# Gate and up groups with three, four or five seven-product pairs, the fifth pair kept in tiles of later activations

## The chip, the cores and the metric

The kernel runs on one core of a Trainium2 chip. The metric is device time in microseconds (us). Three runs before the change took 2402.5, 2402.4 and 2402.98 us; their median is 2402.5 us.

## The reference, cut to what matters

The program is a two-layer decoder trunk on 256 tokens with 2048 features in float32: a retention layer and an MLA layer, each followed by a SwiGLU block. The change touches only the first product of SwiGLU:

```
def swiglu(x, w_gu, w_down):
    gate, up = jnp.split(x @ w_gu, [D_FF], axis=-1)      # x: 256 x 2048, w_gu: 2048 x 11264
    return (jax.nn.silu(gate) * up) @ w_down              # D_FF = 5632
```

## The kernel before, in words

Every float32 operand is split into a rounded part (`hi`) and a remainder (`lo`), both in a format that TensorE takes at full speed, and a product is the sum of three matmuls: hi by hi, hi by lo, lo by hi. ScalarE writes `hi` (a cast, L210), VectorE subtracts to get `lo` (L211).

The gate and up product of a layer runs in 11 groups, j = 0 to 10. A group takes 512 columns of gate and 512 of up against all 2048 rows of the weight, which are 16 row tiles of 128, and writes four banks of PSUM: two token halves (t = 0, 1) by two column halves. In the plain form each row tile costs 2 x 2 x 3 = 12 matmuls of 512 columns. Two neighbouring row tiles and the two column halves are a 2 x 2 block product, and for some such pairs of row tiles the Strassen-Winograd form is used: seven block products in place of eight, so 21 matmuls in place of 24, for four more additions of weights on VectorE and four of activations. Group 0 is plain. Groups 1 to 10 go through `first_sevens` with `GU_SEVENS` = 4: pairs 0 to 3 (row tiles 0 to 7) with seven products, row tiles 8 to 15 plain.

`first_sevens` makes, for each pair p, four weight operands: `b` (b00 beside the sum t2, L458 and L459, cast and subtracted in two halves of 512), `a` (the sums ta, L458 and L462, 1024), `c` (the pair's second row tile as loaded, 1024) and `d` (t2 plus a block, L473, 512; two pairs share one tile). TensorE walks them in four loops: per pair b, b, a, a; then c on bank b00; then c on bank b01; then d on bank b10. Between loop one and loop three VectorE turns the banks around: u = b01 + copy of b00 (L485), v = b10 + u (L488), b01 = b11 - u (L492), b11 = b11 - copy of v (L495). The products of c on b01 must wait for L492.

Casts and remainders lie in two rings of five tiles each (tags `whi`, `wlo`, WB = 5); a sixth operand can only be cast when TensorE has used up the first. Row tiles as loaded lie in four `raw` tiles (the first row tile of a pair, s0, and the plain row tiles) and four `y4` tiles (the second row tile of a pair, s1). All loads of 512 KB each are issued by SyncE (the SP queue), in order: one whose buffer is not free holds up those behind it.

The block's activations lie in 11 tiles of tag `aT`, one per group, each written after its group. Until then `spare_a` lends them out: `share(slots, room)` gives a group up to two raw tiles (names with `xraw`) and up to two hi/lo pairs (`xhi`, `xlo`) for its last row tiles, fewer when fewer slots are left.

The left operands of the pairs (sums of activations, L246 to L249 and a split) are made during group 0 by `watched`, when the transposed input of both token halves is there; they are kept for all groups of the layer. The order on each engine is set when the program is built, by the tile framework's scheduler, and the engines follow it in order.

The lines that matter below: L450, L453, L555 (loads of s0, s1, plain row tiles), L456 (t2), L458 to L463 (sums and splits of b and a), L468 (c), L473 (d), L481 and L489 (copies of banks by ScalarE), L485 to L495, L419 (all matmuls), L1005 (`share`).

Of the kernel before, what the change touches and what calls it, by code (L numbers as in the profile page):

```python
# [8 lines left out]
F32 = mybir.dt.float32  # L9
F32R = mybir.dt.float32r  # L10
# [5 lines left out]
P = 128  # L16
SEQ = 256
D = 2048
DT = D // P
# [12 lines left out]
NG = 104  # L32


GU_SEVENS = 4
DN_SEVENS = (2, 5, 7, 10, 12, 15, 17), (2, 4, 5, 7, 10, 12, 15, 17)
RTO_SEVENS = (3, 6, 9, 12), (3, 5, 6, 9, 12)
MLO_SEVENS = (3, 5), (1, 3)
# [20 lines left out]
def trunk(  # L59
# [362 lines left out]
                )  # L422
                begun.add(bank)

    def first_sevens(lhs, kts, w, g, name, n, left, spare):

# [18 lines left out]
        def begin(p):  # L447
            step()
            raw = wp.tile([P, 1024], F32, tag="raw", bufs=RAW, name=f"{name}_s0")
            nc.sync.dma_start(out=raw, in_=w[g, 2 * p])  # L450
            step()
            raw1[p] = r1 = sb.tile([P, 1024], F32, tag="y4", bufs=4, name=f"{name}_s1")
            nc.sync.dma_start(out=r1, in_=w[g, 2 * p + 1])  # L453
            b00, b01, b11 = raw[:, 0:512], raw[:, 512:1024], r1[:, 512:1024]
            ta = tp7.tile([P, 1024], F32, tag="tsum", bufs=2, name=f"{name}_ta")
            t2[p] = wp.tile([P, 512], F32, tag="mv", bufs=MV, name=f"{name}_t2")  # L456
            b, a = parts("b"), parts("a")
            nc.vector.tensor_add(out=ta[:, 0:512], in0=b00, in1=b01)  # L458
            nc.vector.tensor_add(out=t2[p], in0=ta[:, 0:512], in1=b11)  # L459
            split(*half(b, 0), b00)  # L460
            split(*half(b, 1), t2[p])
            nc.vector.tensor_add(out=ta[:, 512:1024], in0=b01, in1=b11)  # L462
            split(*a, ta)  # L463
            wt["b", p], wt["a", p] = b, a
# [116 lines left out]
    def watched(pairs):  # L581


        made, held, tiles = {}, {}, [None]

        def seen(t, k0, n, part):
            for p in range(pairs):
                if k0 <= 2 * p < k0 + n:
                    held[t, p] = part[:, 2 * p - k0], part[:, 2 * p - k0 + 1]
                    if (1 - t, p) in held:  # L590
                        f, hi, lo = tiles[0](len(made))
                        left_sums(*held[0, p], *held[1, p], f, hi, lo)
                        made[p] = hi, lo

        watch[0] = seen
        return made, tiles
# [167 lines left out]
    def retention():  # L764
# [43 lines left out]
        with tc.tile_pool(name="rt_s", bufs=1) as sp:  # L808
# [88 lines left out]
            with tc.tile_pool(name="rt_v", bufs=1) as rp:  # L897
# [63 lines left out]
                    for t in range(NT):  # L961
                        later(2 + t, lambda h=h, t=t, pr=(ph, pl), v=(vh, vl), sg=sg: mixed(h, t, pr, v, sg))

                gu_next[0] = watched(GU_SEVENS)
                closing(
                    take_y, RH * 4, ret_out, g_mix_post[0], G_FFN, "rto",
                    lambda name: rp.tile([P, 1024], F32, tag="sg", bufs=1, name=name), sevens=RTO_SEVENS,
# [3 lines left out]
    def swiglu(i):  # L971
        with tc.tile_pool(name=f"ff{i}", bufs=1) as fp:
# [19 lines left out]

            def sums(n):
                f = wp.tile([P, 4, P], F32, tag="mv", bufs=MV, name=f"sf{i}")
                if n < 2:
                    hi = fp.tile([P, 4, P], F32R, tag="sa", bufs=4, name=f"sh{i}")
                    lo = fp.tile([P, 4, P], F32R, tag="sa", bufs=4, name=f"sl{i}")
                else:
                    hi = wp.tile([P, 4, P], F32R, tag="ah", bufs=3, name=f"sh{i}")
                    lo = wp.tile([P, 4, P], F32R, tag="al", bufs=3, name=f"sl{i}")  # L1000
                return f, hi, lo
# [3 lines left out]

            for j in range(groups):
                name = f"gu{i}_{j}"
                spare = share(groups - j, spare_a)
                if j:
                    banks = first_sevens(  # L1010
                        h_lhs, DT, w_gu[i], j, name, GU_SEVENS, lambda p: ins[p], spare
                    )
                else:
                    banks = group(h_lhs, DT, tile_load(w_gu[i], j, name, 0, spare), name, lead=4)
# [17 lines left out]
    def mla():  # L1032
        with tc.tile_pool(name="ml", bufs=1) as mp:
# [152 lines left out]
            with tc.tile_pool(name="ml_a", bufs=1) as ap:  # L1186
# [110 lines left out]
                for hp in range(AH // 2):  # L1297
                    if hp:
                        qb = pair_products(hp)
                    attention(hp, qb)  # L1300
                gu_next[0] = watched(GU_SEVENS)
                closing(
                    lambda k0, n: oT[:, k0 : k0 + n], AH, mla_out, g_mix_post[1], G_FFN + DT, "mlo",
                    lambda name: ap.tile([P, 1024], F32, tag="aqkT", bufs=1, name=name), sevens=MLO_SEVENS,
# [98 lines left out]
```

## Time and profile before

| what | value |
|---|---|
| profiled execution, own time | 2400.07 us |
| its span, first to last instruction | 2398.3 us |
| median of the three runs | 2402.5 us |
| granted TensorE clock, mean | 0.999 |
| TensorE busy (matmuls) | 2382.3 us, 99% |
| VectorE busy | 2179.7 us, 91% |
| ScalarE busy | 1500.3 us, 63% |

Times in the trace count from the first instruction of the span. A matmul's recorded time is longer than the distance to the next one, since they are pipelined; distances between starts are what counts. In a timeline, a row with `xN` merges N instructions, and the bracket names the idle time of the engine before the row and what ended it.

### The profile page before, as it was taken

Reading aid. Unit: us, or ns where it says so; the run is one execution under the profiler, and the core shown is the slowest. Engines: PE = TensorE matmul, PEld = TensorE weight load, DVE = VectorE, ACT = ScalarE, POOL = GpSimd, SP = SyncE. Lnnn points to the kernel's source line nnn. Section 1 sums busy time; section 2 is a strip of 40 time slices with the busy share of each in tenths; the row PEclk is TensorE's granted clock in tenths of the full one; section 3 lists DMA queues with packets and bytes.
Section 4 is the critical chain, followed back from the end, with each engine's and each line's share of the span. In section 5 each row is a group of like instructions: output and inputs, shape, how many; then the busy total and the mean of one; then the engine's idle time right before and its main releaser. Section 6 shows DMA issues by size and latency. Waiting matters only on the chain.

```text
span 2398.3 us, 30805 instructions
## 1 busy us (share of the span) xinstructions
PE 2382.3 (99%) x10843; PEld 1971.0 (82%) x10843; DVE 2179.7 (91%) x3112; ACT 1500.3 (63%) x2126; POOL 28.5 (1%) x38
## 2 busy tenths in 40 slices
PE   9999999999999999999999999999999999999998
PEld 7888888888888888888888888887888888888887
DVE  8899888888899999999988987889999999998998
ACT  6555665665666656666666666656666665666664
POOL 0000000000000000000000000000100000000000
PEclk9999999999999999999999999999999999999999
DMA  8555465545656665656456655445666565645655
GB/s 285 187 195 191 167 212 184 170 170 192 206 194 219 207 207 199 209 179 219 161 197 210 200 196 158 129 138 171 234 205 216 177 218 184 212 167 183 221 199 168
DMA packets 129611, 463.76 MB, mean 193 GB/s; under 512 B 14640, under 2 KB 15024, under 8 KB 129456
## 3 DMA queue, kind: packets, MB, share of 16 engines
q1 hardware_dynamic: 129456, 461.80, 57.7%
q8 instruction: 85, 1.39, 0.2%
q14 instruction: 70, 0.57, 0.1%
HBM read 459.64 MB, written 2.10 MB: 193 GB/s over the span
## 4 chain that ended last, share of the span: by engine, by line
PE 94%; DVE 4%; DMA 1%; issue 1%; ACT 1%; SPq 0%; POOL 0%; DVEq 0%; POOLq 0%; ACTq 0%
PE gu_b L419 37%; PE dn_b L419 15%; PE rvg_b L419 14%; PE rqk_b L419 6%; PE rto_b L419 6%; PE q L419 3%; PE dn_m L419 3%; PE mlo_b L419 2%; PE mc_b L419 1%; PE rto_m L419 1%; PE ftp L988 1%; PE ry L916 1%; PE htp L602 0%; PE rsc L861 0%; PE asc L1240 0%
## 5 line engine op out<-in xcount | busy, mean ns | idle before, releaser
L419 PE MATMUL gu_b<-gu_w_hi,hT 128*128 128x512 f32 x1296 | 353.6, 391 | 0.1
L419 PEld LDWEIGHTS gu_b<-gu_w_hi,hT 128*128 128x128 f32 x1296 | 242.3, 188 | 50.6 <-DVE hT L211 0.9
L210 ACT CAST dn_w_hi<-dn_w_raw 128x1024 fp32r<-128x1024 f32 (+1 forms) x176 | 169.1, 978 | 78.4 <-DMA dn_w_raw<-w_down 33.7
L419 PE MATMUL gu_b<-gu_w_lo,hT 128*128 128x512 f32 x648 | 200.4, 391 | 0.0
L211 DVE TENSOR_TENSOR dn_w_lo<-dn_w_raw,dn_w_hi 128x1024 fp32r<-128x1024 f32 (+1 forms) x176 | 193.8, 1130 | 7.1 <-ACT dn_w_hi L210 6.3
L419 PE MATMUL rvg_b<-rvg_w_hi,hT 128*128 128x512 f32 x576 | 157.4, 391 | 0.0
L419 PE MATMUL dn_b<-dn_w_lo,dn_ah 128*128 128x512 f32 x494 | 156.7, 390 | 0.3 <-DVE dn_w_lo L211 0.3
L419 PE MATMUL dn_b<-dn_w_hi,dn_ah 128*128 128x512 f32 x494 | 156.7, 390 | 0.0
L419 PE MATMUL dn_b<-dn_w_hi,dn_al 128*128 128x512 f32 x494 | 156.7, 390 | 0.0
L211 DVE TENSOR_TENSOR gu_w_lo<-gu_w_raw,gu_w_hi 128x1024 fp32r<-128x1024 f32 x122 | 143.6, 1223 | 6.0 <-ACT gu_w_hi L210 6.0
L419 PEld LDWEIGHTS gu_b<-gu_w_lo,hT 128*128 128x128 f32 x648 | 121.2, 188 | 26.3 <-DVE gu_w_lo L211 1.5
L210 ACT CAST gu_w_hi<-gu_w_raw 128x1024 fp32r<-128x1024 f32 x122 | 122.5, 1049 | 29.2 <-PE gu_b L419 11.3
L419 PEld LDWEIGHTS rvg_b<-rvg_w_hi,hT 128*128 128x128 f32 x576 | 107.7, 188 | 22.0
L210 ACT CAST gu_ahi<-gu_ta 128x1024 fp32r<-128x1024 f32 x80 | 84.4, 1055 | 46.7 <-PE gu_b L419 36.0
L211 DVE TENSOR_TENSOR gu_clo<-gu_s,gu_chi 128x1024 fp32r<-128x1024 f32 x80 | 97.6, 1222 | 14.7 <-ACT gu_chi L210 13.4
L419 PEld LDWEIGHTS dn_b<-dn_w_lo,dn_ah 128*128 128x128 f32 x494 | 92.7, 188 | 19.8 <-DVE dn_w_lo L211 0.7
L419 PEld LDWEIGHTS dn_b<-dn_w_hi,dn_ah 128*128 128x128 f32 x494 | 92.8, 188 | 19.2
L419 PEld LDWEIGHTS dn_b<-dn_w_hi,dn_al 128*128 128x128 f32 x494 | 92.8, 188 | 19.2
L211 DVE TENSOR_TENSOR gu_alo<-gu_ta,gu_ahi 128x1024 fp32r<-128x1024 f32 x80 | 97.8, 1223 | 7.0 <-ACT gu_ahi L210 6.9
L210 ACT CAST gu_bhi<-gu_s 128x512 fp32r<-128x512 f32 x80 | 49.7, 622 | 81.6 <-PE gu_b L419 65.9
L419 PE MATMUL rqk_b<-rqk_w_hi,hT 128*128 128x512 f32 x352 | 99.4, 396 | 1.2 <-ACT rqk_w_hi L210 1.1
L210 ACT CAST gu_chi<-gu_s 128x1024 fp32r<-128x1024 f32 x80 | 83.8, 1051 | 13.6 <-PE gu_b L419 13.4
(535 smaller groups left out, 6284.9 us busy)
## 6 DMA issues: line engine op xcount, KB each, us to landing
dn_w_raw<-w_down SPq DMA_DIRECT2D x176, 512.0 KB, 4.5
gu_s<-w_gu SPq DMA_DIRECT2D x160, 512.0 KB, 4.6
gu_w_raw<-w_gu SPq DMA_DIRECT2D x152, 512.0 KB, 3.7
rvg_w_raw<-ret_vg SPq DMA_DIRECT2D x67, 512.0 KB, 4.4
rto_w_raw<-ret_out SPq DMA_DIRECT2D x64, 512.0 KB, 4.3
rvg_s<-ret_vg SPq DMA_DIRECT2D x48, 512.0 KB, 4.2
rqk_w_raw<-ret_qk SPq DMA_DIRECT2D x43, 512.0 KB, 4.3
gu_w_xraw<-w_gu SPq DMA_DIRECT2D x40, 512.0 KB, 5.2
```

Source lines behind the costliest of these rows:

```text
L210: nc.scalar.copy(out=hi, in_=src)
L211: nc.vector.tensor_sub(out=lo, in0=src, in1=hi.bitcast(F32))
L419: nc.tensor.matmul(out, e[2](), e[3](), start=bank not in begun, stop=ends[bank, added.get(bank, 0)] == n, skip_group_check=bank in added,)
L916: nc.tensor.matmul(y, left, right, start=n == 0, stop=n == len(terms) - 1)
L988: nc.tensor.transpose(tp[:, b * P : (b + 1) * P], a[:, b * P : (b + 1) * P], ident)
```

## The change

`GU_SEVENS` becomes a list by group: none in group 0, three pairs in group 1, then 5, 4, 5, 4, 5, 4, 4, 4, 4. Over a layer's groups 1 to 10 that is 42 pairs where there were 40. In a group with five pairs, the second row tile and t2 of pair 4 lie in `aT` tiles, and so do the left operands of pair 4, from group 0 until group 6. `kept` takes these out of what `share` may lend.

```diff
-GU_SEVENS = 4
+GU_SEVENS = 0, 3, 5, 4, 5, 4, 5, 4, 4, 4, 4
...
-    def first_sevens(lhs, kts, w, g, name, n, left, spare):
+    def first_sevens(lhs, kts, w, g, name, n, left, spare, fifth=None):
...
-            raw1[p] = r1 = sb.tile([P, 1024], F32, tag="y4", bufs=4, name=f"{name}_s1")
+            if p < 4:
+                raw1[p] = sb.tile([P, 1024], F32, tag="y4", bufs=4, name=f"{name}_s1")
+            else:
+                raw1[p] = fifth(F32, f"{name}_s1")
+            r1 = raw1[p]
             nc.sync.dma_start(out=r1, in_=w[g, 2 * p + 1])
...
-            t2[p] = wp.tile([P, 512], F32, tag="mv", bufs=MV, name=f"{name}_t2")
+            if p < 4:
+                t2[p] = wp.tile([P, 512], F32, tag="mv", bufs=MV, name=f"{name}_t2")
+            else:
+                t2[p] = fifth(F32, f"{name}_t2")[:, 0:512]
...
-                gu_next[0] = watched(GU_SEVENS)
+                gu_next[0] = watched(max(GU_SEVENS))
...
             def sums(n):
                 f = wp.tile([P, 4, P], F32, tag="mv", bufs=MV, name=f"sf{i}")
-                if n < 2:
+                if n == 4:
+                    both = spare_a(F32R, f"s{i}").rearrange("p (n j q) -> p n j q", n=2, j=4)
+                    hi, lo = both[:, 0], both[:, 1]
+                elif n < 2:
...
-                spare = share(groups - j, spare_a)
+
+                kept = int(j and max(GU_SEVENS[j:]) > 4) + 2 * (GU_SEVENS[j] > 4)
+                spare = share(groups - j - kept, spare_a)
                 if j:
                     banks = first_sevens(
-                        h_lhs, DT, w_gu[i], j, name, GU_SEVENS, lambda p: ins[p], spare
+                        h_lhs, DT, w_gu[i], j, name, GU_SEVENS[j], lambda p: ins[p], spare, spare_a
                     )
```

Counted over the whole program, TensorE has 183 matmuls of 512 columns in group 1, 177 in groups 2, 4 and 6, and 180 in the others from 1 to 10, where all ten had 180. Lines of the kernel after the change are numbered 8 to 13 higher than those named above: L450 becomes L451, L453 L458, L555 L563, L459 L467, L462 L470, L473 L481, L485 L493, L488 L496, L492 L500, L495 L503.

The places that follow are in group 2 of layer 0 (`gu0_2`), in the order in which each engine takes its instructions; groups 4 and 6 and layer 1 have the same pattern. First the loads on SyncE, before:

```order
L450 DMA gu0_2_s0_7517<-w_gu 128x1024
L450 DMA gu0_2_s0_7554<-w_gu 128x1024
L555 DMA gu0_2_w8_raw_7664<-w_gu 128x1024
L555 DMA gu0_2_w9_raw_7682<-w_gu 128x1024
L555 DMA gu0_2_w10_raw_7700<-w_gu 128x1024
L555 DMA gu0_2_w11_raw_7718<-w_gu 128x1024
L555 DMA gu0_2_w12_xraw_7736<-w_gu 128x1024
```

And the loads on SyncE now:

```order
L451 DMA gu0_2_s0_7551<-w_gu 128x1024
L451 DMA gu0_2_s0_7582<-w_gu 128x1024
L563 DMA gu0_2_w10_raw_7710<-w_gu 128x1024
L563 DMA gu0_2_w11_raw_7728<-w_gu 128x1024
L563 DMA gu0_2_w14_raw_7782<-w_gu 128x1024
L458 DMA gu0_2_s1_7584<-w_gu 128x1024
L563 DMA gu0_2_w12_xraw_7746<-w_gu 128x1024
L563 DMA gu0_2_w13_xraw_7764<-w_gu 128x1024
```

`s0_7582` and `s1_7584` are the two row tiles of the fifth pair. The first goes into the raw tile that pair 0 left, so the plain row tiles move one raw tile on, and `w14_raw` takes the raw tile of pair 3's first row tile (`s0_7551`), which `w11_raw` took before (that of `s0_7554`). The fifth pair's second row tile stands right behind it.

Next VectorE, around the end of loop one, before (`clo` is the remainder of c, `mv1` is u, and the writes to `b10`, `b01`, `b11` are L488, L492, L495):

```order
L211 TENSOR_TENSOR gu0_2_alo_7563<-gu0_2_ta_7558,gu0_2_ahi_7562 128x1024
L211 TENSOR_TENSOR gu0_2_clo_7597<-gu0_2_s1_7453,gu0_2_chi_7596 128x1024
L211 TENSOR_TENSOR gu0_2_clo_7604<-gu0_2_s1_7481,gu0_2_chi_7603 128x1024
L485 TENSOR_TENSOR gu0_2_mv1_7581<-gu0_2_b01_7448,gu0_2_mv0_7576 128x512
L211 TENSOR_TENSOR gu0_2_clo_7611<-gu0_2_s1_7525,gu0_2_chi_7610 128x1024
L488 TENSOR_TENSOR gu0_2_b10_7449<-gu0_2_b10_7449,gu0_2_mv1_7581 128x512
L492 TENSOR_TENSOR gu0_2_b01_7448<-gu0_2_b11_7450,gu0_2_mv1_7581 128x512
L211 TENSOR_TENSOR gu0_2_clo_7618<-gu0_2_s1_7556,gu0_2_chi_7617 128x1024
```

And VectorE now, from the fifth pair's `b` on:

```order
L211 TENSOR_TENSOR gu0_2_blo_7589<-gu0_2_s0_7582,gu0_2_bhi_7588 128x512
L467 TENSOR_TENSOR gu0_2_t2_7587<-gu0_2_ta_7586,gu0_2_s1_7584 128x512
L470 TENSOR_TENSOR gu0_2_ta_7586<-gu0_2_s0_7582,gu0_2_s1_7584 128x512
L211 TENSOR_TENSOR gu0_2_blo_7589<-gu0_2_t2_7587,gu0_2_bhi_7588 128x512
L481 TENSOR_TENSOR gu0_2_t2_7587<-gu0_2_t2_7587,gu0_2_s1_7584 128x512
L211 TENSOR_TENSOR gu0_2_alo_7591<-gu0_2_ta_7586,gu0_2_ahi_7590 128x1024
L493 TENSOR_TENSOR gu0_2_mv1_7609<-gu0_2_b01_7445,gu0_2_mv0_7604 128x512
L211 TENSOR_TENSOR gu0_2_clo_7625<-gu0_2_s1_7450,gu0_2_chi_7624 128x1024
L496 TENSOR_TENSOR gu0_2_b10_7446<-gu0_2_b10_7446,gu0_2_mv1_7609 128x512
L500 TENSOR_TENSOR gu0_2_b01_7445<-gu0_2_b11_7447,gu0_2_mv1_7609 128x512
L211 TENSOR_TENSOR gu0_2_clo_7632<-gu0_2_s1_7478,gu0_2_chi_7631 128x1024
L503 TENSOR_TENSOR gu0_2_b11_7447<-gu0_2_b11_7447,gu0_2_mv0_7604 128x512
```

Before, two remainders of c stood ahead of u and a third ahead of v; now the first stands behind u, and the second behind L500.

Last TensorE at the start of loop two, before:

```order
L419 MATMUL gu0_2_b11_7450<-gu0_2_ahi_7562,sl0_6788 128x512
L419 MATMUL gu0_2_b00_7447<-gu0_2_chi_7596,hT_6599 128x512
L419 MATMUL gu0_2_b00_7447<-gu0_2_clo_7597,hT_6599 128x512
L419 MATMUL gu0_2_b00_7447<-gu0_2_chi_7596,hT_6599 128x512
L419 MATMUL gu0_2_b00_7447<-gu0_2_chi_7603,hT_6599 128x512
```

And TensorE now, from the fifth pair's last products on:

```order
L419 MATMUL gu0_2_b00_7444<-gu0_2_chi_7624,hT_6599 128x512
L419 MATMUL gu0_2_b10_7446<-gu0_2_alo_7591,s0_6855 128x512
L419 MATMUL gu0_2_b10_7446<-gu0_2_ahi_7590,s0_6855 128x512
L419 MATMUL gu0_2_b11_7447<-gu0_2_alo_7591,s0_6855 128x512
L419 MATMUL gu0_2_b11_7447<-gu0_2_ahi_7590,s0_6855 128x512
L419 MATMUL gu0_2_b00_7444<-gu0_2_clo_7625,hT_6599 128x512
L419 MATMUL gu0_2_b00_7444<-gu0_2_chi_7624,hT_6599 128x512
L419 MATMUL gu0_2_b00_7444<-gu0_2_chi_7631,hT_6599 128x512
L419 MATMUL gu0_2_b01_7445<-gu0_2_chi_7624,sh0_6705 128x512
L419 MATMUL gu0_2_b01_7445<-gu0_2_clo_7625,sh0_6705 128x512
L419 MATMUL gu0_2_b01_7445<-gu0_2_chi_7624,sl0_6706 128x512
L419 MATMUL gu0_2_b01_7445<-gu0_2_chi_7631,sh0_6722 128x512
```

The fifth pair's products with `alo` are moved behind the first product of c, and the products of c on b01 now begin after four matmuls of loop two, where ten stood ahead of them before. Counting from the first product of pair 4's block (the fifth pair) as number 0, the product with its second `blo` is number 4, that with `alo` number 12, the first with `clo` number 16, the first on b01 number 19, the one with the second `clo` number 23 and the one with the third number 30.

## Rows read from the trace of the kernel before

**Rows 1.** From the page: the span, the engines' busy time, and the chain of work that ended last, by engine; a group of casts (its count, busy us, mean ns); and a group of loads (count, size, median us to landing).

```profile
span 2398.3 us, 30805 instructions
...
PE 2382.3 (99%) x10843; PEld 1971.0 (82%) x10843; DVE 2179.7 (91%) x3112; ACT 1500.3 (63%) x2126; POOL 28.5 (1%) x38
...
PE 94%; DVE 4%; DMA 1%; issue 1%; ACT 1%; SPq 0%; POOL 0%; DVEq 0%; POOLq 0%; ACTq 0%
...
L210 ACT CAST gu_bhi<-gu_s 128x512 fp32r<-128x512 f32 x80 | 49.7, 622 | 81.6 <-PE gu_b L419 65.9
...
gu_w_xraw<-w_gu SPq DMA_DIRECT2D x40, 512.0 KB, 5.2
```

**Rows 2.** Busy time of each engine (and its instructions) in stretches of one gate and up group each: groups 1, 3, 4 and 9 of layer 0 and group 1 of layer 1. The first column is the stretch, the second its length; then PE, PEld, DVE, ACT and POOL, the granted clock, the DMA share and GB/s.

```profile
775.30:816.80 41.50, 40.58 (x182) 33.03 (x181) 41.39 (x56) 26.95 (x37) 0.00 (x0) 1.00 0.64 207
...
858.60:900.30 41.70, 41.70 (x189) 34.61 (x188) 39.44 (x52) 26.63 (x34) 0.00 (x0) 1.00 0.60 202
900.30:942.10 41.80, 41.80 (x189) 34.64 (x189) 39.44 (x52) 26.64 (x34) 0.00 (x0) 1.00 0.61 200
...
1109.00:1150.80 41.80, 41.80 (x191) 34.67 (x190) 38.50 (x51) 25.49 (x34) 0.00 (x0) 1.00 0.59 196
...
1742.50:1782.50 40.00, 39.56 (x178) 32.38 (x177) 40.00 (x53) 27.02 (x35) 0.00 (x0) 1.00 0.65 216
```

**Rows 3.** The timeline of the first half of group 4 of layer 0, all engines, a selection in order of time: start, length, engine, line, operation. Its first product starts at 901.71.

```profile
901.44 0.75 DVE L1021 SCALAR_TENSOR_TENSOR fa<-gu_b,rto_x_r,fsg 128x512 f32<-128x512 f32 x1
...
901.71 0.39 PE L419 MATMUL gu_b<-gu_bhi,hT 128*128 128x512 f32 x1
...
904.40 1.23 DVE L211 TENSOR_TENSOR gu_alo<-gu_ta,gu_ahi 128x1024 fp32r<-128x1024 f32 x1 [0.95 <-ACT gu_ahi L210]
...
906.01 0.69 DVE L211 TENSOR_TENSOR gu_blo<-gu_s,gu_bhi 128x512 fp32r<-128x512 f32 x1 [0.38 <-ACT gu_bhi L210]
...
906.67 1.06 ACT L210 CAST gu_ahi<-gu_ta 128x1024 fp32r<-128x1024 f32 x1 [0.17 <-PE gu_b L419]
906.73 0.33 SPq L555 DMA_DIRECT2D gu_w_raw<-w_gu  x1
907.11 0.90 SPq L555 DMA_DIRECT2D gu_w_xraw<-w_gu  x2
...
908.50 0.39 PE L419 MATMUL gu_b<-gu_bhi,sl 128*128 128x512 f32 x1
...
908.98 1.05 ACT L210 CAST gu_chi<-gu_s 128x1024 fp32r<-128x1024 f32 x1 [0.29 <-PE gu_b L419]
...
910.06 2.54 DVE L211 TENSOR_TENSOR gu_clo<-gu_s,gu_chi 128x1024 fp32r<-128x1024 f32 x2 [0.90 <-ACT gu_chi L210]
910.09 0.39 PE L419 MATMUL gu_b<-gu_bhi,hT 128*128 128x512 f32 x1
...
911.25 0.58 ACT L481 COPY gu_mv<-gu_b 128x512 f32<-128x512 f32 x1
...
913.49 0.39 PE L419 MATMUL gu_b<-gu_chi,hT 128*128 128x512 f32 x1
...
914.85 0.69 DVE L492 TENSOR_TENSOR gu_b<-gu_b,gu_mv 128x512 f32<-128x512 f32 x1
...
915.76 0.40 PE L419 MATMUL gu_b<-gu_chi,sh 128*128 128x512 f32 x1
...
917.18 2.49 DVE L211 TENSOR_TENSOR gu_dlo<-gu_t,gu_dhi 128x512 fp32r<-128x512 f32 x4
...
919.59 4.63 DVE L211 TENSOR_TENSOR gu_w_lo<-gu_w_raw,gu_w_hi 128x1024 fp32r<-128x1024 f32 x4
```

**Rows 4.** The view of DMA issues for 907.05 to 907.45, which holds the load issued at 906.73 and the first of the two issued at 907.11: tile, queue, number, size, us from issue to landing.

```profile
gu_w_raw<-w_gu SPq DMA_DIRECT2D x1, 512.0 KB, 3.8
gu_w_xraw<-w_gu SPq DMA_DIRECT2D x1, 512.0 KB, 4.6
```

**Rows 5.** TensorE's timeline in group 1 of layer 0, the two rows with idle time.

```profile
788.49 0.50 PE L419 MATMUL gu_b<-gu_clo,hT 128*128 128x512 f32 x1 [0.69 <-DVE gu_clo L211]
...
789.70 0.50 PE L419 MATMUL gu_b<-gu_chi,sh 128*128 128x512 f32 x1 [0.23 <-DVE gu_b L492]
```

**Rows 6.** The view of waits of TensorE's weight loads (PEld) over the whole program, three of its rows: who waited for whom, total us, times, longest.

```profile
PEld gu_b L419 <- DVE gu_w_lo L211: 1.5, 4, 0.5
...
PEld gu_b L419 <- DVE gu_clo L211: 1.1, 1, 1.1
PEld gu_b L419 <- DVE gu_b L492: 1.0, 2, 0.7
```

**Rows 7.** VectorE's timeline in group 0 of layer 0: one addition and one split of the left operands, and two later rows with idle time.

```profile
742.88 0.29 DVE L247 TENSOR_TENSOR sf<-sf,hx 128x128 f32<-128x128 f32 x1
743.08 0.29 DVE L248 TENSOR_TENSOR sf<-hx,hx 128x128 f32<-128x128 f32 x1
...
744.69 0.69 DVE L211 TENSOR_TENSOR sl<-sf,sh 128x512 fp32r<-128x512 f32 x1
...
762.83 0.69 DVE L458 TENSOR_TENSOR gu_ta<-gu_s 128x512 f32<-128x512 f32 x1 [0.28 <-DMA gu_s<-w_gu]
764.49 1.23 DVE L211 TENSOR_TENSOR gu_w_xlo<-gu_w_raw,gu_w_xhi 128x1024 fp32r<-128x1024 f32 x1 [0.97 <-ACT gu_w_xhi L210]
```

More of the change, by code (lines that the diff above doesn't have):

```diff
@@ L1300, in mla @@
                     attention(hp, qb)
-                gu_next[0] = watched(GU_SEVENS)
+                gu_next[0] = watched(max(GU_SEVENS))
                 closing(
```

## The prediction, made before the changed kernel ran

> **What bounds the kernel now.** I read the page first, then busy time by stretches of one group, then the timeline of one group, then loads and waits. TensorE is busy 99% and holds 94% of the chain that ended last; VectorE has 91% of busy time but 4% of the chain [rows 1]. Group by group the same is to be seen: in groups 3, 4 and 9 TensorE has no gap in 41.7 to 41.8 us, while VectorE works 38.5 to 39.4 us and ScalarE 26.6 [rows 2]. From the first product of a pair's block at 910.09 to the first of loop two at 913.49 lie 15 matmuls [rows 3], so one takes 3.40 / 15 = 0.2267 us, and 180 of them with 8 small transposes fill the group. So time falls only if matmuls go, and rises as soon as VectorE is late for one. VectorE's gaps in group 4 are 0.95, 0.38 and 0.90 us, all ahead of remainders that wait for a cast, and the casts wait for TensorE to leave one of the five weight tiles [rows 3]: it runs as far ahead as the ring lets it, and not further.
>
> **Matmuls removed.** Two pairs more per layer (42 for 40) at 3 matmuls each, in two layers: 12 x 0.2267 = 2.7 us less. The Trainium skill (TensorE: Matmul & The Clock Gate, Back-to-back issue gap) gives some 131 ns per 512-column matmul in a sustained stream; by that it would be 1.6 us. The spacing in the trace decides against it here.
>
> **VectorE's work.** A seven-product pair has seven operations of 512 (L458, L459, L462, L473, two `blo`, one `dlo`) and two of 1024 where a plain one has two of 1024. Four `dlo` in a row last 2.49 us, the last recorded 0.69, so one costs (2.49 - 0.69) / 3 = 0.60; four `w_lo` last 4.63, so 1024 cost about 1.13 [rows 3]. A pair more is 7 x 0.60 = 4.2 us. A five-pair group then asks 39.4 + 4.2 = 43.6 us of VectorE and takes TensorE 41.7 - 0.7 = 41.0; with the four-pair group behind it that is 83.0 against 82.7. The gaps of 2.3 us per group are used up, but the balance holds to 0.3 us per couple, which group 1 with 35.2 us against 42.4 and the lead on plain row tiles cover. I take 0.1 us for each of the six four-pair groups behind a five-pair one, 0.6 in all; the bounds are 0 and the whole deficit, 2.6 x 6 = 15.6. ScalarE has three casts more and 15 us free per group: nothing. Groups 4 to 6 lose one or two lent hi/lo pairs; group 9 ran without any and had no gap [rows 2], so nothing, at worst the 0.2 to 0.7 us of a wait like those in [rows 5].
>
> **The fifth pair's second row tile.** Time t counts from a group's first product (901.71 in rows 3). SyncE issues in order. In group 4 the load into the raw tile of pair 3 was issued at 906.73, as the `blo` begun at 906.01 had ended; the next went out at 907.11 [rows 3] and landed 4.6 us later [rows 4], at t = 10.0. Now this place is `w14_raw`, and the next is the fifth pair's s1. VectorE stands one addition later at that `blo` (the L466 of the fifth pair moved ahead of it), so t = 5.15, 5.5 and 10.1. What VectorE does until then, by its order: the remainder of pair 2's a from 2.7 (904.40), addition to 4.4, two `blo` and L481 to 6.25, pair 3's a to 7.4, the fifth pair's first `blo` when its cast is there. That cast needs the ring tile left by the product at 908.50, as the cast at 908.98 did [rows 3]: 7.2 + 0.6, so `blo` ends at 8.4. Then L467 reads s1: VectorE waits 1.7 us, to 10.15, in all six five-pair groups. No row shows such a wait; its bounds are 0 (the load is issued early) and 2.3 (a landing of 5.2 us, the median of the `xraw` loads [rows 1]).
>
> **What is late next.** Behind L467 stand all the steps of the turn from loop one to loop two. L467 to 10.8, L470 to 11.4 while ScalarE casts t2 (0.62 [rows 1], from 10.9); `blo` from 11.55, done at 12.25. Block five starts at t = 910.09 + 12 x 0.2267 - 901.71 = 11.1 and wants it as its number 4, at 12.0: TensorE is held 0.3 us. L481, `alo` to 13.9, done just in time for number 12. Then u to 14.5; the first `clo`, which now stands behind u, done at 15.73, wanted as number 16 at 15.03 (with the 0.3): 0.75 us. v to 16.25, b01 done at 16.95, wanted as number 19 at 16.47: 0.5. Second `clo` done 18.07, wanted 17.9: 0.2. Third 0.15. The fourth is early again. Before, L492 began at 914.85 and was done at 915.54, and the first product on b01 began at 915.76 [rows 3]; ten products of c stood ahead of it, now four. Sum: 0.3 + 0.75 + 0.5 + 0.2 + 0.15, about 1.95 us per five-pair group, 11.7 us in six. With s1 in time the same reckoning starts at u, which has to wait for bank b01 (t = 12.6) and whose follower waits for the cast of c behind the copy of bank b00: first `clo` 0.15, b01 0.5, then 0.25 and 0.15, 1.0 us per group, 6 us in all. So the term lies between 6 and (with the later landing) 6 x 2.3 = 14 us; I take 11.7, since the load's row is an exact match in queue place and size.
>
> **Groups 0 and 1.** The left operands of pair 4 add four additions and one split per layer on VectorE, 4 x 0.20 + 0.60 = 1.4 us [rows 7], in group 0, where remainders of plain row tiles already come late four times [rows 6]; gaps of 0.28 and 0.97 us later in the group [rows 7] take part of it up. Group 1 waited 0.69 and 0.23 us for `clo` and L492 [rows 5], and the whole program shows 1.1 and 1.0 us of such waits [rows 6]; three pairs free 4.2 us of VectorE there, but loop two also falls from 12 to 9 matmuls while the steps from u to L492 stay. I take the two as equal, 0, with bounds of -1.8 (these waits go) and +2 (0.5 per layer in group 0, 0.5 in group 1).
>
> **Sum.** -2.7 + 11.7 + 0.6 + 0 = +9.6 us. Against the profiled execution's own 2400.07 us that is 2409.7; the median of the runs lies 2.4 us above it, so 2412 us.
>
> **Rivals.** First, the load is in time and only the turn is late: -2.7 + 6 + 0 = +3.3, 2406. For it speaks that a 512 KB load landed in 3.8 us when it stood first [rows 4]; against it, that s1 stands second, behind a tile which VectorE frees late. Second, the other side, not slower: TensorE's new order fills the turn. The mechanism is the order of numbers 11 to 19: products of c are drawn ahead of `alo`, and `dhi` products ahead of the last `clo`, so if `clo` and L492 end before 15.0 and 15.4, nothing waits, and -2.7 with up to -1.5 in group 1 gives 2398 to 2400. It decides at t = 15.4, and u, one `clo`, v and L492 from 12.6 need 0.6 + 1.1 + 0.6 + 0.7 = 3.0, which is 0.2 too late even without any cast or load. Third, VectorE becomes the bound and the four-pair groups give nothing back: -2.7 + 15.6 = 2415; against it, the gaps of 2.3 us in each four-pair group [rows 2, 3]. The Trainium skill (VectorE: DVE Perf Modes, The DRAIN you can't avoid) has a Vector operation start only when the one before has left the pipe; by that the seven would cost 7 x 0.69 = 4.8 us, and this rival would come 3.6 us later. The distance of 0.60 between starts speaks against it.
>
> **How the numbers follow.** Forecast 0.55, first rival 0.20, second 0.13, third 0.12. About 0.2% (4.8 us) is what a measurement of this kernel can tell from no change. The forecast (own range 2408 to 2415) and the third rival count as slower, with a few hundredths of the first: 0.70. The rest of the first and the second are the same: 0.28. Faster by over 0.2% would need more than the 2.7 us of matmuls and all waits of group 1 together: 0.02. The range of 8 in 10 goes from 2401, which leaves out most of the second rival, to 2415.
>
> **What would show it.** Right: in the waits, VectorE's L467 waits for a DMA of `gu_s` six times, 1 to 2 us each; TensorE waits for `gu_clo`, `gu_blo` and the bank of L500 some 12 us in all; groups 2, 4 and 6 take about 43.0 us, groups 3 and 5 still 41.7 to 41.8, group 1 42.4 to 43. Wrong: groups 2, 4 and 6 at 41.0 to 41.2 us (second rival), at 42 with no wait for a load (first), or four-pair groups at 43 (third). The L467 row would also be wrong if s1 lands before t = 9.

## The result, and the profile after

The changed kernel takes 2413.3 us (median of five runs, 2409.6 to 2414.7) where the kernel before took 2403.0 us beside it: the ratio is 1.0045 with a 95% interval of 1.0034 to 1.0056. It is slower by 10 us, 0.45%. The prediction was 2412.

The page after, with its span, busy times and the chain that ended last:

```profile
span 2412.9 us, 30869 instructions
...
PE 2390.9 (99%) x10831; PEld 1962.0 (81%) x10831; DVE 2196.9 (91%) x3150; ACT 1505.1 (62%) x2140; POOL 36.2 (2%) x38
...
PE 78%; DVE 12%; DMA 5%; issue 3%; ACT 2%; SPq 0%; POOL 0%; DVEq 0%; POOLq 0%; ACTq 0%
```

The shares of busy time are almost those of [rows 1], and tell little. The chain does: TensorE's part of it fell from 94% to 78%, and VectorE and transfers took its place. The view of waits over the whole program says which (who waited for whom, total us, times, longest):

```profile
PEld gu_b L419 <- DVE gu_clo L211: 9.8, 20, 0.8
DVE gu_t L467 <- DMA gu_s<-w_gu: 9.4, 6, 1.8
PEld gu_b L419 <- DVE gu_b L500: 5.7, 11, 0.7
...
PEld gu_b L419 <- DVE gu_blo L211: 2.7, 6, 0.5
...
PE gu_b L419 <- DVE gu_clo L211: 2.4, 7, 0.4
...
PE gu_b L419 <- DVE gu_b L500: 1.8, 8, 0.2
```

In [rows 6] the same view had 1.1 us for `clo` and 1.0 for the bank. The second row is new: VectorE's L467 waits for a load exactly six times, once in each five-pair group. Here is group 4 of layer 0 in the timeline (columns as in [rows 3]), from its first product to the turn, and the first product of group 5:

```profile
903.98 0.39 PE L419 MATMUL gu_b<-gu_bhi,hT 128*128 128x512 f32 x1
...
908.54 0.68 DVE L211 TENSOR_TENSOR gu_blo<-gu_s,gu_bhi 128x512 fp32r<-128x512 f32 x1
...
909.26 0.33 SPq L563 DMA_DIRECT2D gu_w_raw<-w_gu  x1
909.63 0.43 SPq L458 DMA_DIRECT2D gu_s<-w_gu  x1
...
911.90 0.69 DVE L211 TENSOR_TENSOR gu_blo<-gu_s,gu_bhi 128x512 fp32r<-128x512 f32 x1 [0.21 <-ACT gu_bhi L210]
914.03 0.69 DVE L467 TENSOR_TENSOR gu_t<-gu_ta,gu_s 128x512 f32<-128x512 f32 x1 [1.44 <-DMA gu_s<-w_gu]
...
918.49 1.21 DVE L211 TENSOR_TENSOR gu_clo<-gu_s,gu_chi 128x1024 fp32r<-128x1024 f32 x1
919.76 0.49 PE L419 MATMUL gu_b<-gu_clo,hT 128*128 128x512 f32 x1 [0.37 <-DVE gu_clo L211]
920.22 0.68 DVE L500 TENSOR_TENSOR gu_b<-gu_b,gu_mv 128x512 f32<-128x512 f32 x1
920.96 0.50 PE L419 MATMUL gu_b<-gu_chi,sh 128*128 128x512 f32 x1 [0.25 <-DVE gu_b L500]
...
947.07 0.39 PE L419 MATMUL gu_b<-gu_bhi,hT 128*128 128x512 f32 x1
```

The load of `s1` is issued right behind `w14_raw`, which goes when VectorE has done the `blo` begun at 908.54; VectorE is idle for 1.44 us until it lands, and from 2 us later on TensorE stands for what VectorE now makes late, longest at the two rows with brackets. The group lasts 947.07 - 903.98 = 43.09 us. Lengths of groups in this document are counted like that, from first product to first product:

| kernel, layer 0, us | group 2 (five) | 3 | 4 (five) | 5 | 6 (five) | 7 | 2 to 7 |
|---|---|---|---|---|---|---|---|
| before | 41.79 | 41.74 | 41.79 | 41.73 | 41.73 | 41.73 | 250.5 |
| after | 43.15 | 41.97 | 43.09 | 41.97 | 43.60 | 42.21 | 256.0 |

Layer 1 is the same within 0.06 us per group. Of the 14.6 us between the two profiled spans, groups 2 to 7 hold 5.5 in each layer, groups 0 and 1 hold 0.1 together, and the other 3.6 lie where nothing was changed: 1.0 ahead of the first gate and up product, 0.9 between the last one of layer 0 and the first of layer 1, 1.7 behind the last of layer 1.

### The profile page after: what moved, and what is told of

Its sections match the earlier page's. It is cut to its first block, busy times and chain, and to the rows that moved or that the text cites. A ratio compares the mean times of both kernels' runs of the same rounds, so it can differ in the third digit from the quotient of the medians.

```text
span 2412.9 us, 30869 instructions
## 1 busy us (share of the span) xinstructions
PE 2390.9 (99%) x10831; PEld 1962.0 (81%) x10831; DVE 2196.9 (91%) x3150; ACT 1505.1 (62%) x2140; POOL 36.2 (2%) x38
## 4 chain that ended last, share of the span: by engine, by line
PE 78%; DVE 12%; DMA 5%; issue 3%; ACT 2%; SPq 0%; POOL 0%; DVEq 0%; POOLq 0%; ACTq 0%
PE gu_b L419 25%; PE rvg_b L419 14%; PE dn_b L419 13%; PE rqk_b L419 6%; PE rto_b L419 6%; PE q L419 3%; PE dn_m L419 3%; PE mlo_b L419 2%; DMA gu_s<-w_gu 1%; DVE gu_w_lo L211 1%; PE mc_b L419 1%; DMA dn_w_raw<-w_down 1%; DMA gu_w_raw<-w_gu 1%; PE rto_m L419 1%; DVE gu_blo L211 1%
## 5 line engine op out<-in xcount | busy, mean ns | idle before, releaser
L210 ACT CAST gu_bhi<-gu_t 128x512 fp32r<-128x512 f32 x84 | 52.1, 621 | 75.5 <-DVE gu_t L467 75.3
```

What stands on the lines that cost most here:

```text
L210: nc.scalar.copy(out=hi, in_=src)
```

## The experiments

The expectations on record speak of groups of 43.5 us in the changed kernel: they count from ScalarE's first read of a group's banks, which puts 0.4 us of a four-pair group into the five-pair group ahead of it. All numbers measured are given as in the table above, for layer 0, with the ratio to the kernel before and its 95% interval; where layer 1 differs by more than 0.1 us, the text says so.

**The load early, the half load, the order alone, and no fifth pair.**

`load_early` issues the fifth pair's s1 before everything that waits for VectorE:

```diff
-            else:
-                raw1[p] = fifth(F32, f"{name}_s1")
...
-            nc.sync.dma_start(out=r1, in_=w[g, 2 * p + 1])
...
+        if n > 4:
+            raw1[4] = fifth(F32, f"{name}_s1")
+            nc.sync.dma_start(out=raw1[4], in_=w[g, 9])
         for p in range(n):
```

> The fifth pair's second row tile is loaded right behind the loads of the first two pairs, ahead of every load that waits for VectorE; nothing else in the code is changed, but the orders come out otherwise too: the fifth pair's a products stay ahead of all products of c, and seven products of c instead of four stand ahead of the first on b01. Theory of the prediction (load and turn each cost about half): no wait of L467 for a load is left, groups 2, 4 and 6 go from 43.5 to about 42.1 us, the time from 2413 to 2405 to 2407. Rival 'only the turn': the wait for the load goes and the groups stay at 43 or above, 2411 to 2413. Rival 'VectorE is the bound': the groups come to 42 or less but the four-pair groups behind them rise above 42, 2410 to 2413. Rival 'only the load': groups 2, 4 and 6 at 41.1 to 41.3, 2399 to 2401.

Measured: 2401.7 us, ratio 0.9998 (0.9990 to 1.0007). Groups 2 to 7: 42.10, 41.75, 41.39, 41.85, 41.39, 41.98. The whole loss is gone; the time is three to five us below what the theory of the prediction expected. In group 4 the load goes out 22 us before VectorE's first use of it (L468, which is L470 of the changed kernel), and VectorE waits for no load:

```profile
886.43 0.38 SPq L508 DMA_DIRECT2D gu_s<-w_gu  x1
...
908.69 0.68 DVE L468 TENSOR_TENSOR gu_ta<-gu_s,gu_s 128x512 f32<-128x512 f32 x1
909.29 1.22 DVE L211 TENSOR_TENSOR gu_alo<-gu_ta,gu_ahi 128x1024 fp32r<-128x1024 f32 x1
910.42 0.69 DVE L465 TENSOR_TENSOR gu_t<-gu_ta,gu_s 128x512 f32<-128x512 f32 x1
911.02 0.68 DVE L211 TENSOR_TENSOR gu_blo<-gu_s,gu_bhi 128x512 fp32r<-128x512 f32 x1
```

But not the load alone differs from the changed kernel. TensorE's order does: seven products of c stand ahead of b01 in group 2, and ten, as before the change, in groups 4 and 6 (the expectation on record says seven for all). So does VectorE's: the changed kernel makes one `clo` ahead of the subtraction for b01, load_early three (in group 2 two, and the remainder of a plain row tile). The next two runs try to take these apart.

`half_first` keeps the place in the queue, and splits the load:

```diff
-            nc.sync.dma_start(out=r1, in_=w[g, 2 * p + 1])
...
+                nc.sync.dma_start(out=r1[:, 512:1024], in_=w[g, 2 * p + 1, :, 512:1024])
+                nc.sync.dma_start(out=r1[:, 0:512], in_=w[g, 2 * p + 1, :, 0:512])
```

> The load of the fifth pair's second row tile stays behind the same plain row tile in SyncE's queue, but goes as two loads of 256 KB, first the half that the waiting addition reads. The order of TensorE comes out as in load_early (seven products of c ahead of b01). If the landing sets the time as predicted, the wait of L467 falls from 1.5 us to 0.3 to 0.9 us and groups 2, 4 and 6 come to 42.2 to 42.6 us, 2406 to 2409. If the order on TensorE is what counts, the groups are as in load_early within 0.1 us. If neither counts, 43.5 us and 2413.

Measured: 2411.5 us, 1.0046 (1.0033 to 1.0058), groups 43.30, 41.97, 42.90, 41.97, 43.16, 42.18; in layer 1 the five-pair groups are shorter, 42.63, 42.71 and 42.60. The half came a little sooner. Here is group 4, and the row of the view of waits for all six groups:

```profile
909.96 0.43 SPq L461 DMA_DIRECT2D gu_s<-w_gu  x1
910.43 0.42 SPq L462 DMA_DIRECT2D gu_s<-w_gu  x1
...
914.04 0.69 DVE L471 TENSOR_TENSOR gu_t<-gu_ta,gu_s 128x512 f32<-128x512 f32 x1 [1.13 <-DMA gu_s<-w_gu]
...
DVE gu_t L471 <- DMA gu_s<-w_gu: 5.8, 6, 1.2
```

From issue to use 4.08 us, where the full load took 914.03 - 909.63 = 4.40. The wait fell by 0.3 us in this group, and in all six from 9.4 to 5.8 us, 0.6 per group, the least that was expected; the groups stayed at 42.6 us or more, where 42.2 to 42.6 were expected. TensorE's order, seven products of c ahead of b01 in every five-pair group, did not bring the time of load_early with the load still late. VectorE's order is a third one here, with two `clo` ahead of the subtraction for b01.

`order_only` leaves the load late and VectorE's order as in the changed kernel, and pins TensorE's order to that of load_early's group 2, with seven products of c ahead of b01 (edges of issue order, no waits):

```diff
...
+            plan[b11[3 * n - 1]] += (None, "loop1")
+            for k in b00[3 * n : 3 * n + 3]:
+                plan[k] += ("loop1",)
+            plan[b00[3 * n + 6]] += (None, "c2")
+            for k in b01[3 * n : 3 * n + 3]:
+                plan[k] += ("c2",)
```

> The load stays late; only TensorE's order at the turn of a five-pair group is set as it is in load_early: the fifth pair's a products ahead of all products of c, seven products of c ahead of the first on b01. VectorE's order there stays that of the changed kernel. Theory of the prediction: L467 still waits 1.4 to 1.7 us for the load in all six groups, TensorE is now held for alo (about 0.8 us) and for the first clo (0.2 to 0.5) and no longer for b01; groups 2, 4 and 6 at 42.5 to 42.8 us, 2408 to 2409. Rival 'only the turn's order': groups at 41.5 to 42.0, 2402 to 2405. Rival 'only the load': 43.5, 2413.

Measured: 2417.5 us, 1.0064 (1.0050 to 1.0078), groups 43.98, 41.73, 43.95, 41.73, 44.37, 42.02: slower still, against all three theories (in layer 1 the third five-pair group is 43.96). In group 4 TensorE stands for the first `clo` and then, longer, for the second:

```profile
919.37 0.50 PE L421 MATMUL gu_b<-gu_clo,hT 128*128 128x512 f32 x1 [0.31 <-DVE gu_clo L211]
921.70 0.50 PE L421 MATMUL gu_b<-gu_clo,hT 128*128 128x512 f32 x1 [1.37 <-DVE gu_clo L211]
```

With seven products of c ahead of b01, the second `clo` is wanted before the bank, and VectorE, late by the load, makes it behind the subtraction for the bank. So with the load late and VectorE's order as in the changed kernel, four products of c ahead of b01 are better than seven. That is no rule for a late load: half_first, with seven, one `clo` more ahead of the bank and 0.6 us less to wait for, is 6 us faster than order_only.

`no_five` has three pairs in group 1, four in all others, and still makes the fifth pair's left operands:

```diff
-GU_SEVENS = 0, 3, 5, 4, 5, 4, 5, 4, 4, 4, 4
+GU_SEVENS = 0, 3, 4, 4, 4, 4, 4, 4, 4, 4, 4
...
-                gu_next[0] = watched(max(GU_SEVENS))
+                gu_next[0] = watched(5)
...
-                kept = int(j and max(GU_SEVENS[j:]) > 4) + 2 * (GU_SEVENS[j] > 4)
+                kept = int(0 < j < 7)
```

> Group 1 keeps its three pairs and the left operands of a fifth pair are still made in group 0 (and read by nothing), but groups 2 to 10 have four pairs as before the change. 39 pairs in a layer where the kernel before has 40: 6 matmuls more, 1.4 us. Theory of the prediction (groups 0 and 1 cost nothing beside the matmuls): groups 2 to 10 at 41.7 us, time 2403 + 1.4 = 2404.4. If the sums in group 0 and the shorter second loop of group 1 cost what the bounds allow, up to 2406.4; if the waits of group 1 go, 2402.6. If some of the change's 10 us lies outside the five-pair groups, this kernel shows it: 2407 or more.

Measured: 2401.7 us, 1.0000 (0.9991 to 1.0009), groups 2 to 7 all 41.69 to 41.76. In the trace groups 0 and 1 last 0.4 us longer than before in layer 0 and 1.0 in layer 1, together the 1.4 us of the six matmuls; the median, uncertain by 2 us, does not show them. The loss is in the five-pair groups and behind them.

**The load early in the late load's order, the queue, and the waits that are left.**

`early_four_c` has the load of load_early and, from the fifth pair's first a product to the seventh product of c on b01, TensorE's order of the changed kernel: its plan is rearranged there, and each product pinned behind the one before. VectorE's order is that of load_early.

```diff
...
+            pinned = [k for k in order if plan[k][0] == "mm"]
+            for q, k in enumerate(pinned):
+                plan[k] += (f"o{q - 1}", f"o{q}")
+            plan[:] = plan[:first] + [plan[k] for k in order + rest_of]
```

> Load early as in load_early, but TensorE's order from the fifth pair's first a product on is pinned to that of the changed kernel (the a products behind the first product of c, four products of c ahead of b01). VectorE's order is that of load_early. With order_only this makes the square: load late or early, four or seven products of c ahead. New theory (the late landing alone costs; the scheduler's order is its answer to it): the bank b01 is ready when it is in load_early and wanted three matmuls (0.68 us) sooner, so TensorE is held 0.3 + 0.7 = 1.0 us in groups 4 and 6 and 1.4 to 1.8 in group 2: groups of 42.0 to 42.1 and 42.5 to 42.8 us, 2405 to 2407; no wait of VectorE for a load. Rival (the four-product order is what holds TensorE in the changed kernel): 43.0 or more in all of them, 2410 or more. Rival (with the load in time the order does not matter): as load_early, 2401 to 2402.

Measured: 2408.5 us, 1.0027 (1.0017 to 1.0037), groups 42.77, 41.73, 42.76, 41.75, 42.79, 41.97. No wait for the load, but one for the bank in each five-pair group; in group 4 three `clo` (the first row is two of them) stand ahead of it on VectorE:

```profile
913.83 2.36 DVE L211 TENSOR_TENSOR gu_clo<-gu_s,gu_chi 128x1024 fp32r<-128x1024 f32 x2
...
916.70 1.22 DVE L211 TENSOR_TENSOR gu_clo<-gu_s,gu_chi 128x1024 fp32r<-128x1024 f32 x1
...
918.43 0.69 DVE L502 TENSOR_TENSOR gu_b<-gu_b,gu_mv 128x512 f32<-128x512 f32 x1
...
919.18 0.50 PE L421 MATMUL gu_b<-gu_chi,sh 128*128 128x512 f32 x1 [1.42 <-DVE gu_b L502]
```

The mean of the three five-pair groups in the four kernels, with what VectorE makes ahead of the subtraction for b01:

| | load late (one `clo` ahead) | load early (three remainders ahead) |
|---|---|---|
| four products of c ahead of b01 | 43.28 (after) | 42.77 (early_four_c) |
| seven (load_early: ten in groups 4 and 6) | 44.10 (order_only) | 41.63 (load_early) |

This is not a clean square, since VectorE's order moves with the load. In the two pinned kernels the orders of the two engines do not fit: in order_only TensorE wants a second `clo` that VectorE makes behind the bank, in early_four_c it wants the bank that VectorE makes behind three `clo`. So -0.5 (after to early_four_c) is not the price of the load alone, nor +0.8 (after to order_only) that of an order. Why the scheduler gives each kernel its order is not shown.

`pool_queue` changes the queue: the same place in the program, issued by GpSimd.

```diff
-            nc.sync.dma_start(out=r1, in_=w[g, 2 * p + 1])
+            (nc.sync if p < 4 else nc.gpsimd).dma_start(out=r1, in_=w[g, 2 * p + 1])
```

> The changed kernel, but the load of the fifth pair's second row tile is issued by GpSimd's queue in place of SyncE's, at the same place in the program. If what is late is the place in SyncE's queue behind a load that waits for VectorE: no wait of VectorE for this load, groups 2, 4 and 6 as in load_early (41.4 to 42.2 us), 2401 to 2404. If the transfer itself is slow, or the tile it goes to comes free late: the wait of 1.2 us or more stays, and 2411 or more.

Measured: 2403.5 us, 1.0006 (0.9997 to 1.0014), groups 41.67, 41.96, 41.66, 41.94, 42.09, 42.18 (in layer 1 the third five-pair group is 41.67). In group 4 the load leaves at 884.95, 25 us before its use, and L467 follows the `blo` ahead of it at once:

```profile
884.95 0.55 POOL L458 DMA_DIRECT2D gu_s<-w_gu  x1 [109.25 <-DVE gu_w_lo L211]
...
909.99 0.69 DVE L211 TENSOR_TENSOR gu_blo<-gu_s,gu_bhi 128x512 fp32r<-128x512 f32 x1 [0.21 <-ACT gu_bhi L210]
910.60 0.69 DVE L467 TENSOR_TENSOR gu_t<-gu_ta,gu_s 128x512 f32<-128x512 f32 x1
```

So the tile is free in time; what made the load late was its place behind `w14_raw` in SyncE's queue.

The orders came out otherwise here too, and they happen to be those of half_first: by their names, the instructions of TensorE, VectorE and ScalarE in groups 2 to 7 follow each other in both kernels in the same sequence. So this pair shows what a late load costs with the orders held (half_first also has it in halves). half_first waits for it 0.85 to 1.16 us in each of the six five-pair groups, pool_queue never; the groups last 42.88 us on average over both layers in one and 41.74 in the other, and groups 2 to 7 of both layers 509.6 and 502.7, 6.9 us apart, where the medians are 8.0 us apart.

`early_pinned` adds two pins on VectorE to load_early, `early_pinned_four` a fourth pair in group 1 as well:

```diff
-            split(*wt["c", p], raw1[p])
+            with tc.issue_after(kept["c01"]) if n > 4 and p > 1 else nullcontext():
+                split(*wt["c", p], raw1[p])
...
-            tiles[kt] = load(kt)
+            with tc.issue_after(kept["c01"]) if n > 4 else nullcontext():
+                tiles[kt] = load(kt)
```

> load_early with two pins on VectorE in five-pair groups: the remainders of c from the third on, and those of the plain row tiles, stand behind the subtraction that makes bank b01. In load_early TensorE was held 0.3 us for that bank in groups 4 and 6 and 1.0 us in group 2, where a plain remainder stood ahead of the first clo. If these are the last waits, the six groups come to 41.0 to 41.2 us and the time to 2397.5 to 2399.5. If the pins only move the wait to the third clo: 41.4 and more, 2401 to 2402.

> early_pinned with four pairs instead of three in group 1: 6 matmuls less, 1.4 us. If VectorE has the room in group 1 that the kernel before shows (it made four pairs there with 0.9 us of waits): 1 to 1.5 us under early_pinned. If VectorE enters group 2, now with five pairs, later by what the fourth pair costs it (4.2 us less 2.3 of gaps): TensorE is held 1 to 2 us more there in each layer and the time is 1 to 3 us above early_pinned.

Measured: 2401.8 us for both, 1.0000 and 1.0003 (each 0.0009 either way). The five-pair groups of early_pinned are now 41.25, 41.37 and 41.38 (in layer 1 the third is 42.19), but the groups behind them 41.90, 42.27 and 42.01, and the sum, 250.2 (250.9 in layer 1), is about that of before. With the fourth pair in group 1 it is 251.0. The pins move the waits into the four-pair groups.

**VectorE as the bound.** The busy times of two groups in a row (columns of [rows 2]): before the change groups 3 and 4, both with four pairs, and in early_pinned groups 4 and 5, with five and four:

```profile
859.97:943.49 83.52, 83.52 (x377) 69.25 (x376) 78.90 (x101) 53.28 (x69) 0.00 (x0) 1.00 0.61 202
```

```profile
901.58:985.22 83.64, 83.39 (x374) 68.50 (x373) 82.13 (x107) 54.74 (x72) 0.00 (x0) 1.00 0.57 195
```

VectorE has gone from 78.9 of 83.5 us to 82.1 of 83.6, 98%. `less_vector` takes work from it alone. It leaves out the additions that make the operand d in groups 2 to 7, 27 in a layer, so that part of the product is missing:

```diff
-            nc.vector.tensor_add(out=t2[p], in0=t2[p], in1=raw1[p][:, 0:512])
+            if not (name.startswith("gu") and 2 <= g <= 7):
+                nc.vector.tensor_add(out=t2[p], in0=t2[p], in1=raw1[p][:, 0:512])
```

> early_pinned without the additions that make the fourth operand d in groups 2 to 7 (that part of the computation is left out; d is cast from t2 as it is): 5 or 4 operations of VectorE with 0.60 us each fewer in a group, TensorE and ScalarE do what they did. If VectorE's work is what takes the matmuls' gain back in early_pinned (groups 2 to 7 of a layer last 250.2 to 250.9 us there, 250.5 before the change, and would last 3 x 41.05 + 3 x 41.75 = 248.4 without a wait): 248.4 to 248.8 us per layer, no group above 41.8, and 2397 to 2399. If the waits left in early_pinned come from the orders or from casts alone: the groups stay at 41.4 to 42.2 and the time within 0.5 us of early_pinned.

Measured: 2397.4 us, 0.9985 (0.9976 to 0.9993), groups 41.23, 41.73, 41.24, 41.71, 41.21, 41.79, in sum 248.9.

```profile
900.10:983.05 82.95, 82.95 (x374) 68.58 (x373) 77.22 (x98) 54.73 (x72) 0.00 (x0) 1.00 0.58 197
```

With VectorE at 77.2 us TensorE has no gap in groups 4 and 5, and the removed matmuls show up in the time for the first time. `pool_adds` and `pool_adds_five` try to have that with the whole result, by `nc.gpsimd.tensor_add` in place of the addition left out; the second has four pairs in group 1 and five in groups 2 to 6:

> early_pinned with the additions for d in groups 2 to 7 done by GpSimd in place of VectorE; the result is complete. GpSimd is idle there. If its additions do not hold VectorE up: as less_vector, 2397 to 2399. If the two engines slow each other (VectorE's operations longer than 0.69 us beside them, or starts further apart than 0.60): between that and early_pinned, or slower, 2400 to 2405.

> pool_adds with four pairs in group 1 and five in each of groups 2 to 6: 45 pairs in a layer where the kernel before has 40, 30 matmuls fewer in all, 6.8 us. With 5 x 0.60 us off VectorE, a five-pair group asks it for 43.6 - 3.0 = 40.6 us against 41.05 of TensorE. If that balance holds, 2395 to 2397; if GpSimd's additions hold VectorE up, it falls behind in a row of five-pair groups with no four-pair group between them to catch up: groups 3 to 6 at 42 or more, 2403 or more.

Measured: 2422.1 us, 1.0084 (1.0070 to 1.0098), and 2440.4, 1.0164 (1.0150 to 1.0178). GpSimd's additions hold VectorE up, as in this stretch of pool_adds:

```profile
893.91 2.24 POOL L480 TENSOR_TENSOR gu_t<-gu_t,gu_s 128x512 f32<-128x512 f32 x1 [22.17 <-DMA gu_s<-w_gu]
894.92 1.78 DVE L465 TENSOR_TENSOR gu_t<-gu_ta,gu_s 128x512 f32<-128x512 f32 x1
896.63 0.68 DVE L211 TENSOR_TENSOR gu_blo<-gu_s,gu_bhi 128x512 fp32r<-128x512 f32 x1
```

`dma_adds` lets the transfer add, on GpSimd's queue:

```diff
-            nc.vector.tensor_add(out=t2[p], in0=t2[p], in1=raw1[p][:, 0:512])
+            if name.startswith("gu") and 2 <= g <= 7:
+                nc.gpsimd.dma_start(out=t2[p], in_=w[g, 2 * p + 1, :, 0:512], accum_op=ALU.add)
+            else:
+                nc.vector.tensor_add(out=t2[p], in0=t2[p], in1=raw1[p][:, 0:512])
```

> early_pinned with the additions for d in groups 2 to 7 done by the transfer itself: a load of 256 KB on GpSimd's queue that adds to t2 in place; the result is complete. 27 loads more per layer (6.75 MB). If GpSimd's work for them does not hold VectorE up and they land before the cast of d (1 to 5 us after t2's remainder is done, where d is wanted over 10 us later): as less_vector, 248.9 us for groups 2 to 7 and 2397 to 2399, under both kernels. If GpSimd's writing of the transfers takes VectorE's time as its additions did in pool_adds: VectorE's operations longer than 0.69 us beside them, and 2403 or more. If the loads get in the way of the weights': VectorE and ScalarE wait for loads of gu_s and gu_w_raw, 2401 or more.

Measured: 2400.8 us, 1.0002 (0.9993 to 1.0011), groups 41.25, 41.75, 42.28, 41.73, 41.22, 41.76. VectorE is not slowed, and five of the six groups are those of less_vector. Group 4 is 1.0 us longer (1.5 in layer 1), and its rows tell where (the last two are that load in the view of DMA issues, in dma_adds and in less_vector):

```profile
914.69 1.05 ACT L210 CAST gu_w_xhi<-gu_w_raw 128x1024 fp32r<-128x1024 f32 x1 [1.52 <-DMA gu_w_raw<-w_gu]
...
916.59 0.58 ACT L499 COPY gu_mv<-gu_b 128x512 f32<-128x512 f32 x1
...
917.20 0.70 DVE L505 TENSOR_TENSOR gu_b<-gu_b,gu_mv 128x512 f32<-128x512 f32 x1 [1.08 <-ACT gu_mv L499]
...
gu_w_raw<-w_gu SPq DMA_DIRECT2D x1, 512.0 KB, 6.5
...
gu_w_raw<-w_gu SPq DMA_DIRECT2D x1, 512.0 KB, 4.7
```

ScalarE stands 1.5 us at the cast of a plain row tile whose load is not there, with the turn's copy behind it. It looks like the change's own fault, but it is another one: the load is issued 8.81 us after the group's first product in both kernels, and only takes longer beside the adding loads. In the six five-pair groups this load lands 6.0 to 6.9 us after its issue, against 4.1 to 5.2 in less_vector. In groups 2 and 6 ScalarE has this cast behind the copy, and they are not longer. Without these 2.5 us dma_adds would come to some 2398 us, by estimate; that was not tried. No version with the whole result is faster than the kernel before.

## Why the prediction was right, step by step

**Right: the place of the load.** Counted from the first product (903.98), the prediction had `w14_raw` issued at t = 5.15, s1 at 5.5 and usable at 10.1, the `blo` ahead of L467 done at 8.4 and a wait of 1.7. Measured: 5.28, 5.65, 10.05, 8.61 and 1.44. Six waits, 9.4 us in all.

**Right: what is late next, in size.** The five holds of TensorE in group 4 were reckoned as 0.3, 0.75, 0.5, 0.2 and 0.15, together 1.95 us. By the distances between starts beyond 0.227, they are 0.27 (`blo`), 0.65 (first `clo`), 0.52 (b01), 0.21 and 0.12; together 1.77. A sixth hold makes it 1.95: 0.18 at number 11, the first product of c, whose weight load waited 0.34 us for ScalarE's cast, a wait that the prediction did not have. That the two sums agree is chance.

**Mis-sized: the sum over the groups.** With 41.05 us for 177 products, the six five-pair groups hold 259.7 - 246.3 = 13.4 us of waits, where 11.7 were taken: groups 2 and 4 have 2.0 to 2.1, group 6, with a load wait of up to 1.8, has 2.55. The four-pair groups behind them take 1.9 us more than before (0.2 to 0.3 in groups 3 and 5, 0.4 to 0.5 in 7), where 0.6 were taken. The 0.6 rested on group 1 asking VectorE for 35.2 us only; the rows do not show that room: VectorE was busy 41.4 of 41.5 us there before [rows 2], and 41.1 of 42.9 after the change. Groups 0 and 1 come to +0.1 with 1.4 us of matmuls in it, so their waits gave back 1.3, inside the bounds of -1.8 and +2 and not the 0 taken. In all -2.7 + 13.4 + 1.9 - 1.3 = 11.3 against +9.6 forecast, and 10.3 between the medians. It is partly luck that 2412 lies 1.3 us from the median: two terms were 1.7 and 1.3 us too small and one 1.3 too large. Of the signs on record, group 1 (42.85) and the six waits came as told; groups 3 and 5 took 41.97 us and not 41.7 to 41.8, and the waits of weight loads for `clo`, `blo` and the bank come to 18.2 us and not some 12.

**Wrong: the turn with the load in time.** The prediction held that with s1 in time a group would still lose 1.0 us in the turn, and priced its first rival at 2406. load_early gave 2401.7, with 0.34 us of waits in groups 4 and 6 (1.05 in group 2, where the remainder of a plain row tile stands ahead of the first `clo`), and pool_queue 2403.5, with 0.6 us in five of its six groups. The step that failed kept the orders of the changed kernel on both engines while it moved the load; in both runs they came out otherwise. What that turn costs with the load in time and both orders kept, no run shows: early_four_c has 1.7 us, but only TensorE's order, with two more `clo` ahead of the bank on VectorE. So the 1.95 us per group cannot be divided into a share of the load and one of the turn; the pair with equal orders gives 1.1 us per group for a load that keeps VectorE waiting 1.0.

**Right as a mechanism, too early: VectorE as the bound.** The third rival did not decide the changed kernel, whose VectorE still idled 256.0 - 246.2 = 9.8 us over groups 2 to 7 (13.7 before), but it decides what lies behind the load. The prediction reckoned 83.0 us of VectorE's work for a couple of groups; early_pinned shows 82.1 of 83.6, and less_vector, without those additions, is 4.0 us under the kernel before, 3.2 of it in groups 2 to 7, where 18 matmuls (4.1 us) are gone. So a load in time made the change harmless; in no run with VectorE's whole work did it make it a gain.

**The second rival,** that TensorE's order fills the turn, was wrong: it was to decide at t = 15.4, and L500 ended at 920.90, t = 16.9 (reckoned 16.95).

## What to carry to other kernels

A new load takes the lateness of whatever stands ahead of it in its in-order queue: look which engine must free that buffer, and whether the queue can be entered earlier or another one used. The rows of an order are good only for the timing they were drawn for; where an experiment moves a load, read the order of every engine again before pricing a term, and look for a pair of kernels that differ in the load alone. And where two engines are both over 90% busy, a trade of one's work for the other's pays only up to the second one's free time: 4.2 us of additions for 0.7 us of matmuls used up VectorE's gaps in each of the six five-pair groups and the groups behind them.

## What the runs showed of the hardware

GpSimd's addition of 128x512 took 1.99 us on average in pool_adds, and VectorE's operations with two inputs in SBUF beside it up to 1.79 us for 0.69; L465 rose from 686 to 803 ns on average, `alo` from 1222 to 1509. In groups 2 to 7 VectorE was busy 253.5 us against 246.0 in early_pinned, though it had 27 additions fewer to do. The Trainium skill (SBUF — State Buffer, SBUF: two separate sides) says that GpSimd and a VectorE operation with two SBUF inputs take turns on one pair of ports and the later one is blocked whole; the rows above agree, since the operation begun at 894.92 ends at 896.70, 0.55 us after GpSimd's (896.15).

The same additions made by the transfer (5.2 us from issue to landing, 256 KB) left VectorE alone: L465 took 683 ns. They did not leave the other loads alone: a 512 KB load issued at the same place took 6.0 to 6.9 us to land instead of 4.1 to 5.2.

In the six five-pair groups a load of 256 KB landed 3.8 to 4.1 us after issue and one of 512 KB, in the same place of the queue, 4.3 to 4.5: cutting this late load in half took 0.6 us from a wait of 1.6, issuing it earlier took all of it.
